# Two-part float16 weights and inputs for the projections, in place of two-part float32r, with the weights scaled by 1024

## The chip, the cores and the metric

The kernel runs on one core of one Trainium2 chip. TensorE (PE in the profile; its weight loads are the row PEld) multiplies, VectorE (DVE) and ScalarE (ACT) work on tiles element by element, GpSimd (POOL) and SyncE (SP) mostly issue transfers (DMA). The metric is the device time of one execution in microseconds (us), the median of several runs.

## The reference, cut to what matters

A sequence of 528 tokens (16 of them meta tokens) with 2048 channels goes through two residual layers. Nearly all of the arithmetic is in four projections, `hn @ w_in` and `... @ w_out` of each layer:

```
for layer in range(DEPTH):                       # DEPTH = 2
    hn = rms_norm(h, norm_gain[layer])
    if layer % 2 == 0:
        y = even_mixer(hn, ...)
    else:
        y = odd_mixer(hn, ...)
    h = h + y
h = rms_norm(h, final_norm_gain)

def even_mixer(hn, w_in, ..., w_out, ...):
    glu_v, glu_g, gate_a, q, c, gate_b, qi, ki, wi = split_last(hn @ w_in, EVEN_SPLITS)
    ...                                          # convolution of width 31; top-k attention of 8 heads
    return jnp.concatenate([a_out, b_out], axis=-1) @ w_out

def odd_mixer(hn, w_in, lb, norm_g, w_out):
    q, fz, i, g = split_last(hn @ w_in, (D_REC, D_REC, D_REC, D_REC))
    ...                                          # gated linear recurrence of 16 heads
    return o @ w_out
```

All inputs and the output are float32.

## The kernel before, in words

**Layout.** Channels lie on the 128 partitions, tokens along the free axis. An input x is 16 tiles of 128 channels by 528 tokens. A weight matrix lies in memory as stripes of 128 output columns; each stripe is two halves of 128 x 1024 float32 (8 blocks of 128 x 128).

**Two parts.** A float32 value is carried as two float32r parts: `hi` is the value as float32r rounds it, `lo` is what is left. For weights `load_half` does it (lines 152 to 161): SP loads a half into `w32` (4 buffers), ACT copies it into `hi` (line 159), DVE subtracts into `lo` (line 160); `wh` and `wl` have 3 buffers each. For inputs `split`, `split2`, `split_tile`, `early_form0`, `gate_form`, `early_form` and `late_form` do the same once per tile. `products` (lines 183 to 191) then multiplies one half: for each of the 8 blocks three products, hi by xh (line 188), hi by xl (line 189) and lo by xh (line 190), all added up in PSUM. A float32r product is one instruction, which loads its own weights; the profile shows the load as a PEld row with the same line.

**Widths.** A stripe over all tokens ("wide") has 2 x 264 columns, one over the 512 tokens without the meta tokens has 512. Three of the projections are done in Strassen's way on blocks of 2 x 2: even output (56 products of one half, 264 columns), and in the odd layer q, part of the gate and the output (147 products of one half, 256 columns). Sums of weight blocks for it are made by adding transfers on POOL's queue (`sum_step`), paced by other work.

**Evacuation.** A wide or narrow stripe leaves PSUM on DVE, multiplied by the row norm (`evac`, line 196). Results of Strassen products are added into their targets on DVE, or copied by ACT (lines 899 to 921, 1034 to 1052, 1395 to 1400 and 1481 to 1512). In the odd layer's Strassen results the norm is multiplied in later (`scaled`, line 991).

**Beside the projections.** While PE multiplies projections, the convolution (line 610, DVE), the choice of the top keys (lines 583 and 584, DVE), attention (lines 675 to 736), and in the odd layer the recurrence of 16 heads (`rec_head`, lines 1148 to 1287) run on the other engines. The recurrence already uses two float16 parts for its small products of 64 columns (lines 1144 to 1146), with weight loads as instructions of their own. Products that are float32 on both sides (transposes, means, attention's values) and the float32r ones of attention's keys (lines 516, 529, 571, 572 and 696) are not part of the projections' path.

**Order.** Each engine works in one fixed order, which a scheduler made from priorities (`band`: weights first, then evacuation, side work, convolution) and its own estimate of times; `issue_after` pins a few places by hand.

**The end.** The last two pairs of output products are followed by the final norm. `final(0)` scales the first 256 tokens group by group (line 1457) into tiles of the pool `r1` (line 1443, 32 of them), which SP sends out, and `final(1)` does the other 256 tokens after the last product.

Of the kernel before, what the change touches and what calls it, by code (L numbers as in the profile page):

```python
# [37 lines left out]
KS, QS = 2.0 ** 14, 1.0  # L38

# [33 lines left out]
def trunk_kernel(ctx: ExitStack, tc: tile.TileContext, x: bass.AP, w: bass.AP, wukv: bass.AP,  # L73
# [78 lines left out]
    def load_half(src, pool=wpool, names=("wh", "wl"), bufs=3, m=128):  # L152
# [6 lines left out]
        halved[:] = [S.activation(uh, used, AF.Copy),  # L159
                     V.tensor_tensor(ul, used, uh.bitcast(F32), op=OP.subtract)]  # L160
# [32 lines left out]
    def evac(dst, parts, rstd):  # L193
        o = T - dst.shape[-1]
        for p, sl in parts:
            V.tensor_tensor(dst[:, sl.start - o:sl.stop - o], p[:dst.shape[0]], rstd[:dst.shape[0], sl],  # L196
                            op=OP.mult)

    def split2(hi, lo, src, scale=1.0):

        if scale == 1.0:
            S.activation(hi, src, AF.Copy)
            V.tensor_tensor(lo, src, hi.bitcast(F32), op=OP.subtract)
        else:
            S.activation(hi, src, AF.Copy, scale=scale)
            V.scalar_tensor_tensor(lo, src, scale, hi.bitcast(F32), op0=OP.mult, op1=OP.subtract)

    def split(pool, src, scale, gname="xh", lname="xl", n=T, bufs=KT):

        xh = pool.tile([128, T], F32R, name=gname, bufs=bufs)  # L210
        xl = pool.tile([128, T], F32R, name=lname, bufs=bufs)
        S.activation(xh[:, T - n:], src, AF.Identity, scale=scale)
        V.scalar_tensor_tensor(xl[:, T - n:], src, scale, xh[:, T - n:].bitcast(F32),
# [134 lines left out]
    def split_tile(k):  # L348
# [3 lines left out]
        xh = r1p.tile([128, T], F32R, name="xh", bufs=KT)  # L352
        xl = r1p.tile([128, T], F32R, name="xl", bufs=KT)
        g = col(V_G0 + k)
        in_turn("a", lambda: S.activation(xh, hin, AF.Identity, scale=g))
        in_turn("v", lambda: V.scalar_tensor_tensor(xl, hin, g, xh.bitcast(F32), op0=OP.mult, op1=OP.subtract))
# [3 lines left out]
    def split_weights(s, half, part=None):  # L360

        m = KWM if s == S_KW else 128
        if part in (None, 0):
            w32 = wpool.tile([128, 1024], F32, name="w32", bufs=4)
            if s == S_KW:
                hi, lo = [et([128, 5, 128], F32, *(("Vt", 3), ("pt", 2))[half]).rearrange("p a b -> p (a b)")
                          .bitcast(F32R) for _ in range(2)]
            else:
                hi, lo = [wpool.tile([128, 1040], F32R, name=n, bufs=3)[:, :1024] for n in ("wh", "wl")]
# [6 lines left out]
        in_turn("a", lambda: S.activation(hi[:, cs], w32[:, cs], AF.Copy))  # L376
        in_turn("v", lambda: V.tensor_tensor(lo[:, cs], w32[:, cs], hi[:, cs].bitcast(F32), op=OP.subtract))
# [71 lines left out]
    with band(SIDE):  # L449
# [4 lines left out]
        V.tensor_scalar(wiT.rearrange("p a b -> p (a b)"), p[:, :NB * NM], 1.0 / 32, None, op0=OP.mult)  # L454
# [30 lines left out]
    with band(SIDE):  # L485
        rc = et([128, T], F32, "acc", 2)
        rstd_from(mean_bcast(ones_d, csq, None), rc, eps_r, et([128, T], F32, "sq", 3), D / 256, eps_c)
        for j in range(2):
            V.scalar_tensor_tensor(cn[j], cn[j], col(V_KV + j), rc, op0=OP.mult, op1=OP.mult)
            CX.append(split(E, cn[j], 1.0, "ch", "cl", bufs=2))  # L490
# [335 lines left out]
    def early_form0(name, src, scale):  # L826
        hi, lo = [xfp.tile([128, HT], F32R, name=n, bufs=24) for n in ("fh", "fl")]
# [8 lines left out]
    with band(SIDE):  # L836
# [6 lines left out]
        for name in ("N2", "N1", "T3", "T4"):  # L843
            for _ in range(4):
                hl = [r1p.tile([128, T], F32R, name=n, bufs=KT) for n in ("xh", "xl")]
# [37 lines left out]
    with band(EVAC):  # L883
# [3 lines left out]
        for n in range(8, KT):  # L887
            residual(n)
    us = [halves_of[p // 2][:, p % 2 * HT:(p % 2 + 1) * HT] for p in range(8)]
    turns = [(p, m) for m in (2, 3, 1, 6, 5, 7, 4) for p in range(8)]  # L890
    for at, (pr, m) in enumerate(turns):
# [5 lines left out]
        with band(EVAC):  # L897
            if m == 2:
                V.tensor_tensor(c0[:, LT], c0[:, LT], o, op=OP.add)
            elif m == 3:  # L900
                V.tensor_tensor(c0[:, RT], c0[:, RT], o, op=OP.add)
            elif m == 1:
                S.activation(u, o, AF.Copy)
                if pr % 3 == 1:
                    paced_steps(lsteps, 1, o, epools["ec"])
                V.tensor_tensor(c0[:, LT], c0[:, LT], o, op=OP.add)
            elif m == 6:
                V.tensor_tensor(u, u, o, op=OP.add)
# [3 lines left out]
            elif m == 5:  # L912
                V.tensor_tensor(c0[:, RT], c0[:, RT], o, op=OP.add)
                V.tensor_tensor(c1[:, RT], c1[:, RT], o, op=OP.subtract)
                finish1(pr)
            elif m == 7:
                V.tensor_tensor(u, u, o, op=OP.add)
                both = c1.rearrange("p (c t) -> p c t", c=2)
                V.tensor_tensor(both, both, u[:, None, :].to_broadcast([128, 2, HT]), op=OP.subtract)
            else:  # L920
                V.tensor_tensor(c1[:, LT], c1[:, LT], o, op=OP.subtract)
# [685 lines left out]
```

## Time and profile before

| what | value |
|---|---|
| median of 3 runs | 1862.81 us (1862.80 to 1863.81) |
| profiled execution | span 1859.9 us from its first to its last instruction; the page gives no other time of it, so the 2.9 us up to the median are taken as what lies around the span |
| mean granted TensorE clock | 0.998 |
| busy share of DVE, ACT, POOL | 81%, 51%, 14% |
| float32r projection products of 128 x 1024 halves, three lines | 12,552 of the lines 188 to 190, and 192 of the lines 412 to 414 |
| weight halves split on ACT and DVE (lines 159 and 160) | 376 |
| bytes moved by DMA | 379.64 MB, 204 GB/s over the span |

How to read it: PE's records overlap, since a product's record lasts some 280 ns while the next starts after some 120 ns. So what a product costs is the distance from one start to the next in a stream without gaps, and not the length of its record; the timeline gives these starts. On DVE and ACT a record's length is close to the cost (neighbouring records overlap a little). The chain that ended last tells which engine's work fills the span.

### The profile page before, as it was taken

The page shows a single profiled execution, that of the slowest core. Times are in us where ns is not written, and L with a number is a line of the kernel's source. Part 1 is how long each engine was busy: PE and PEld are TensorE (multiplying, and loading weights), DVE is VectorE, ACT ScalarE, POOL GpSimd, SP SyncE. Part 2 cuts the span into 40 slices and gives each one's busy share as a digit, 9 for nine tenths or more (in the row PEclk, how much of TensorE's full clock was granted, in tenths as well). Part 3 has the DMA queues.
Part 4 walks back from the last instruction along what each step waited for, and adds up shares of the span by engine and source line. Part 5 has one row for each costly group of instructions (what it writes and reads, how often), then busy time and mean ns, then how long its engine had stood idle before and what let it go on. Part 6 is the DMA issues. An engine that isn't in the chain of part 4 may idle for free.

```text
span 1859.9 us, 39100 instructions
## 1 busy us (share of the span) xinstructions
PE 1847.7 (99%) x15739; PEld 1804.7 (97%) x15739; DVE 1498.6 (81%) x2898; ACT 945.1 (51%) x1719; POOL 264.9 (14%) x469
## 2 busy tenths in 40 slices
PE   9999999999999999999999999999999999999997
PEld 9998899999999999999999999999999999989997
DVE  7699799998658579588876667999899888869777
ACT  6333532234443655456644455766556656546653
POOL 1120132123331212010000001011101110000000
PEclk9999999999999999999999999999999999999999
DMA  7478777988996867786889886655555455325665
GB/s 283 145 245 257 194 230 191 246 219 204 235 262 207 205 196 251 219 264 235 242 253 288 270 252 207 183 155 159 148 152 167 123 159 141 111 94 161 218 223 170
DMA packets 106020, 379.64 MB, mean 204 GB/s; under 512 B 15472, under 2 KB 23320, under 8 KB 103984
## 3 DMA queue, kind: packets, MB, share of 16 engines
q1 hardware_dynamic: 71872, 232.68, 36.4%
q0 software_dynamic: 33680, 144.28, 32.6%
q8 instruction: 123, 2.02, 0.4%
q14 instruction: 57, 0.47, 0.1%
q10 hardware_dynamic: 288, 0.19, 0.0%
HBM read 354.26 MB, written 136.53 MB: 264 GB/s over the span
## 4 chain that ended last, share of the span: by engine, by line
PE 98%; DVE 1%; ACT 0%; DMA 0%; issue 0%; SPq 0%; DVEq 0%
PE mps L188 22%; PE mps L189 22%; PE mps L190 22%; PE s L189 3%; PE s L188 3%; PE s L190 3%; PE sv L189 2%; PE sv L190 2%; PE sv L188 2%; PE st L189 1%; PE st L188 1%; PE st L190 1%; PE po L724 1%; PE s L1144 1%; PE po L1267 1%; PE s L1146 1%
## 5 line engine op out<-in xcount | busy, mean ns | idle before, releaser
L188 PE MATMUL mps<-xh,wh 128*128 128x264 f32 (+2 forms) x2840 | 837.1, 295 | 0.0
L189 PE MATMUL mps<-xl,wh 128*128 128x264 f32 (+2 forms) x2840 | 835.8, 294 | 0.0
L190 PE MATMUL mps<-xh,wl 128*128 128x264 f32 (+2 forms) x2840 | 835.7, 294 | 0.0
L159 ACT ACTIVATE wh<-w 128x1024 fp32r<-128x1024 f32 x376 | 398.5, 1060 | 535.9 <-PE mps L189 351.0
L160 DVE TENSOR_TENSOR wl<-w,wh 128x1024 fp32r<-128x1024 f32 x376 | 459.7, 1223 | 159.9 <-ACT wh L159 155.3
L189 PEld LDWEIGHTS mps<-xl,wh 128*128 128x128 f32 x2840 | 535.0, 188 | 9.2
L188 PEld LDWEIGHTS mps<-xh,wh 128*128 128x128 f32 x2840 | 534.7, 188 | 9.3
L190 PEld LDWEIGHTS mps<-xh,wl 128*128 128x128 f32 x2840 | 534.6, 188 | 9.2
L610 DVE SCALAR_TENSOR_TENSOR z<-u,vec,z 128x528 f32<-128x528 f32 x240 | 180.9, 763 | 2.4
L260 POOL DMA_DIRECT2D ws<-in_w_dram x116 | 104.6, 1108 | 119.4 <-DMA ws<-ws 69.7
L189 PE MATMUL s<-xl,wh 128*128 128x256 f32 (+1 forms) x288 | 81.4, 283 | 0.0
L188 PE MATMUL s<-xh,wh 128*128 128x256 f32 (+1 forms) x288 | 81.4, 282 | 0.0
L190 PE MATMUL s<-xh,wl 128*128 128x256 f32 (+1 forms) x288 | 80.9, 281 | 0.0
L1227 DVE COPY_PREDICATED A<-msk,s 128x256 f32<-128x256 uint8 x96 | 47.0, 489 | 10.2 <-PE s L1146 9.7
L189 PEld LDWEIGHTS s<-xl,wh 128*128 128x128 f32 x288 | 54.2, 188 | 0.7 <-issue 0.6
L190 PEld LDWEIGHTS s<-xh,wl 128*128 128x128 f32 x288 | 54.3, 189 | 0.0
L188 PEld LDWEIGHTS s<-xh,wh 128*128 128x128 f32 x288 | 54.3, 188 | 0.0
L673 POOL DMA_DIRECT2D L<-mask x32 | 31.8, 993 | 148.6 <-DMA L<-bdram 75.6
L1140 ACT ACTIVATE qhm<-q 128x256 f16<-128x256 f32 x96 | 38.4, 416 | 26.2 <-DVE q L1242 16.1
L1140 ACT ACTIVATE kt0h<-k 128x512 f16<-128x512 f32 (+1 forms) x64 | 33.1, 517 | 32.7 <-DVE k L1233 27.0
L196 DVE TENSOR_TENSOR gt<-mps,rstd 128x264 f32<-128x264 f32 (+1 forms) x70 | 31.4, 450 | 21.3 <-PE mps L190 21.0
L302 POOL MEMSET pace<- 128x1 f32 x36 | 3.9, 108 | 298.2 <-ACT pace L301 298.2
(764 smaller groups left out, 4060.1 us busy)
## 6 DMA issues: line engine op xcount, KB each, us to landing
w<-in_w_dram SPq DMA_DIRECT2D x262, 512.0 KB, 4.4
ws<-in_w_dram POOLq DMA_DIRECT2D x158, 512.0 KB, 7.8
w<-ws SPq DMA_DIRECT2D x116, 512.0 KB, 4.3
ws<-ws POOLq DMA_DIRECT2D x58, 512.0 KB, 5.5
ws<-in_w_dram SPq DMA_DIRECT2D x16, 512.0 KB, 7.1
on<-h1d SPq DMA_DIRECT2D x30, 256.0 KB, 4.1
sq<-mbd POOLq DMA_DIRECT2D x16, 264.0 KB, 3.2
qd<-on SPq DMA_DIRECT2D x12, 256.0 KB, 5.4
```

The costliest lines, as they stand in the source:

```text
L159: halved[:] = [S.activation(uh, used, AF.Copy), V.tensor_tensor(ul, used, uh.bitcast(F32), op=OP.subtract)]
L160: V.tensor_tensor(ul, used, uh.bitcast(F32), op=OP.subtract)]
L188: P.matmul(o, hi[:, ws], xh, start=start and k == 0, stop=False)
L189: P.matmul(o, hi[:, ws], xl, start=False, stop=False)
L190: issued.append(P.matmul(o, lo[:, ws], xh, start=False, stop=stop and k == len(X) - 1))
L196: V.tensor_tensor(dst[:, sl.start - o:sl.stop - o], p[:dst.shape[0]], rstd[:dst.shape[0], sl], op=OP.mult)
L260: return G.dma_start(wsum[pair, m], src, accum_op=OP.add, max_dma_last_dim=4096)
L610: V.scalar_tensor_tensor(z, u[:, j:j + T], col(V_CW + i * CW + j), z, op0=OP.mult, op1=OP.add)
L673: return G.dma_start(biased[h, t][:, :wk(t)], M[t], accum_op=OP.add)
L724: P.matmul(o[:, 128 * t:128 * (t + 1)], Vt[:, j, :], pt[:, j, :], start=j == 0, stop=j == t + 1)
L1140: S.activation(hi, src, AF.Copy, scale=scale)
L1227: V.copy_predicated(A.rearrange("p b (n a m) -> p b n a m", a=2, m=mm)[:, :, :, 1, :], msk[:, li - 1 + i:li + i, :].rearrange("p b (n m) - ...
```

## The change

Both parts of the projections' weights and inputs become float16. Weights are multiplied by 1024 as they are split (`WS`, in ACT's copy and in DVE's subtraction, which becomes SCALAR_TENSOR_TENSOR), and each place that reads a projection's result out of PSUM multiplies by 1/1024 (`IW`). Inputs of the projections are split into float16 without a further scale. The keys and values of attention (`CX`, `kih`, `qa`) stay float32r.

```
+WS = 2.0 ** 10
+IW = 1.0 / WS
...
-        hi = pool.tile([128, wide], F32R, name=names[0], bufs=bufs)[:, :1024]
-        lo = pool.tile([128, wide], F32R, name=names[1], bufs=bufs)[:, :1024]
+        hi = pool.tile([128, wide], F16, name=names[0], bufs=bufs)[:, :1024]
+        lo = pool.tile([128, wide], F16, name=names[1], bufs=bufs)[:, :1024]
...
-        halved[:] = [S.activation(uh, used, AF.Copy),
-                     V.tensor_tensor(ul, used, uh.bitcast(F32), op=OP.subtract)]
+        halved[:] = [S.activation(uh, used, AF.Copy, scale=WS),
+                     V.scalar_tensor_tensor(ul, used, WS, uh, op0=OP.mult, op1=OP.subtract)]
...
     def evac(dst, parts, rstd):
...
-            V.tensor_tensor(dst[:, sl.start - o:sl.stop - o], p[:dst.shape[0]], rstd[:dst.shape[0], sl],
-                            op=OP.mult)
+            V.scalar_tensor_tensor(dst[:, sl.start - o:sl.stop - o], p[:dst.shape[0]], IW,
+                                   rstd[:dst.shape[0], sl], op0=OP.mult, op1=OP.mult)
...
+    def gain(to, ps, by=IW):
+        return V.scalar_tensor_tensor(to, ps, by, to, op0=OP.mult, op1=OP.add)
...
-                V.tensor_tensor(c0[:, LT], c0[:, LT], o, op=OP.add)
+                gain(c0[:, LT], o)
...
-                o = r1p.tile([128, T], F32R, name=("xh", "xl")[g % 2], bufs=KT).bitcast(F32)
+                o = fp.tile([128, 2 * HS], F32, name="oc", bufs=4)
```

The other splits (`split`, `split2`, `split_tile`, `split_weights`, `early_form0`, `gate_form`, `early_form`, `late_form`) change their tiles from F32R to F16 in the same way, and the other additions of results become `gain`. Lines shift: 160 of before is 162 now, 188 to 190 are 190 to 192, 196 is 198, 583 and 584 are 589 and 590, 610 is 616, and 1144 to 1146 are 1153 to 1155.

**On PE**, a float16 product does not load its own weights: a LDWEIGHTS instruction stands ahead of each. Here is a place in the recurrence before, where PE comes back from a short float16 pair of a head (`kt0h` holds that head's keys, `s_14878` is its PSUM tile) to the projections:

```order
L1144 LDWEIGHTS kt0h
L1144 MATMUL s_14878<-qlm,kt0h 128x64
L1145 LDWEIGHTS kt0h
L1145 MATMUL s_14878<-qhm,kt0h 128x64
L189 MATMUL mps<-xl,wh 128x264
L190 MATMUL mps<-xh,wl 128x264
L188 MATMUL mps<-xh,wh 128x264
L189 MATMUL mps<-xl,wh 128x264
```

The same return in another head, of the changed kernel:

```order
L1153 LDWEIGHTS kt0h
L1153 MATMUL s_14399<-qlm,kt0h 128x64
L1154 LDWEIGHTS kt0h
L1154 MATMUL s_14399<-qhm,kt0h 128x64
L190 LDWEIGHTS wh
L190 MATMUL mps<-xh,wh 128x264
L191 LDWEIGHTS wh
L191 MATMUL mps<-xl,wh 128x264
L192 LDWEIGHTS wl
L192 MATMUL mps<-xh,wl 128x264
```

The projections now have the same form as the short products beside them, and 12,744 LDWEIGHTS are added (14,280 in all, 1,536 before); the number of products stays at 15,392. There are 58 such returns in the order before and 59 now. The side work stands at nearly the same place among the projections: from the top-k scores to the end of attention at the very same product, elsewhere within some 60 products.

**On DVE**, the order stays as it was through nearly all of the even layer's attention and convolution. Here is a piece of before from the stretch where convolution (`z`), choice of the top keys (`mask`), weight splits (`wl`) and evacuation (`gt`) share the engine:

```order
L160 TENSOR_TENSOR wl<-w_3757,wh 128x1024
L610 SCALAR_TENSOR_TENSOR z<-u,vec,z 128x528
L584 MATCH_REPLACE mask_703<-m_2970,mask_703 128x272
L610 SCALAR_TENSOR_TENSOR z<-u,vec,z 128x528
L196 TENSOR_TENSOR gt<-mps,rstd 128x264
L583 MAX m_2973<-mask_703 128x8
```

The same place in the changed kernel:

```order
L162 SCALAR_TENSOR_TENSOR wl<-w_3757,wh 128x1024
L616 SCALAR_TENSOR_TENSOR z<-u,vec,z 128x528
L590 MATCH_REPLACE mask_703<-m_2970,mask_703 128x272
L616 SCALAR_TENSOR_TENSOR z<-u,vec,z 128x528
L198 SCALAR_TENSOR_TENSOR gt<-mps,rstd 128x264
L589 MAX m_2973<-mask_703 128x8
```

Only the operation of the split and of the evacuation has changed. Over the program 701 TENSOR_TENSOR of DVE become SCALAR_TENSOR_TENSOR. ACT has the same instructions and two more loads of an activation table (11 for 9), because some small operations of the odd layer's set-up (lines 1103 to 1124 of before) now stand earlier, among the even layer's output products.

More of the change, by code (lines that the diff above doesn't have):

```diff
@@ L202, in split2, with split @@
             S.activation(hi, src, AF.Copy)
[L203 removed]
+            V.tensor_tensor(lo, src, plain(hi), op=OP.subtract)
         else:
             S.activation(hi, src, AF.Copy, scale=scale)
[L206 to L211, printed above, removed]
+            V.scalar_tensor_tensor(lo, src, scale, plain(hi), op0=OP.mult, op1=OP.subtract)
+    def split(pool, src, scale, gname="xh", lname="xl", n=T, bufs=KT, dt=F16):
+        xh = pool.tile([128, T], dt, name=gname, bufs=bufs)
+        xl = pool.tile([128, T], dt, name=lname, bufs=bufs)
         S.activation(xh[:, T - n:], src, AF.Identity, scale=scale)
[L213 removed]
+        V.scalar_tensor_tensor(xl[:, T - n:], src, scale, plain(xh[:, T - n:]),
                                op0=OP.mult, op1=OP.subtract)
@@ L366, in split_weights @@
                 hi, lo = [et([128, 5, 128], F32, *(("Vt", 3), ("pt", 2))[half]).rearrange("p a b -> p (a b)")
-                          .bitcast(F32R) for _ in range(2)]
+                          .bitcast(F16)[:, :640] for _ in range(2)]
             else:
-                hi, lo = [wpool.tile([128, 1040], F32R, name=n, bufs=3)[:, :1024] for n in ("wh", "wl")]
+                hi, lo = [wpool.tile([128, 1040], F16, name=n, bufs=3)[:, :1024] for n in ("wh", "wl")]
             first[s, half] = hi, lo
@@ L826, in early_form0 @@
     def early_form0(name, src, scale):
-        hi, lo = [xfp.tile([128, HT], F32R, name=n, bufs=24) for n in ("fh", "fl")]
+        hi, lo = [xfp.tile([128, HT], F16, name=n, bufs=24) for n in ("fh", "fl")]
         split2(hi, lo, src, scale)
@@ L844, in trunk_kernel @@
             for _ in range(4):
-                hl = [r1p.tile([128, T], F32R, name=n, bufs=KT) for n in ("xh", "xl")]
+                hl = [r1p.tile([128, T], F16, name=n, bufs=KT) for n in ("xh", "xl")]
                 forms0[name] += [[t[:, c] for t in hl] for c in (LT, RT)]
@@ L1317, in early_form @@
     def early_form(name, i, src):
-        both = fp.tile([128, 2 * HS], F32R, name=f"{name}{i}", bufs=1)
+        both = fp.tile([128, 2 * HS], F16, name=f"{name}{i}", bufs=1)
         hi, lo = both[:, :HS], both[:, HS:]
@@ L1325, in late_form @@
         if i % 2 == 0:
-            late[name] = [r1p.tile([128, T], F32R, name=n, bufs=KT) for n in ("xh", "xl")]
+            late[name] = [r1p.tile([128, T], F16, name=n, bufs=KT) for n in ("xh", "xl")]
         sl = slice(i % 2 * HS, (i % 2 + 1) * HS)
```

57 lines of the change are left out of this document (30 added, 27 removed).

## The prediction, made before the changed kernel had run

> **What bounds the kernel now.** I read the page's head first, then the chain that ended last, then what PE waited for.
>
> ```profile
> span 1859.9 us, 39100 instructions
> PE 1847.7 (99%) x15739; PEld 1804.7 (97%) x15739; DVE 1498.6 (81%) x2898; ACT 945.1 (51%) x1719; POOL 264.9 (14%) x469
> ...
> PEclk9999999999999999999999999999999999999999
> ...
> PE 98%; DVE 1%; ACT 0%; DMA 0%; issue 0%; SPq 0%; DVEq 0%
> ```
>
> PE fills 98% of the chain at a clock that is never throttled. The list of PE's waits has three entries in all:
>
> ```profile
> PE mps L139 <- DVE ones_d L124: 1.1, 1, 1.1
> PE po L1433 <- DVE rstd L1415: 0.5, 1, 0.5
> PE mps L413 <- DVE xl L356: 0.4, 1, 0.4
> ```
>
> 2 us of waits in 1860: PE is the bound from the first 30 us to the last 12. A busy PE is no proof of that, since its records overlap; that it never waits is. So the distance from one product's start to the next sets the time. Two windows of 100 us hold nothing but projections, the first of 264 columns, the second of 256 (columns: PE, PEld, DVE, ACT, POOL busy with instructions, clock, DMA share, GB/s):
>
> ```profile
> 700.00:800.00 100.00, 100.00 (x826) 100.00 (x825) 75.92 (x133) 49.22 (x82) 14.23 (x28) 1.00 0.78 240
> 1000.00:1100.00 100.00, 100.00 (x853) 100.00 (x853) 59.57 (x75) 44.30 (x68) 9.06 (x24) 1.00 0.87 268
> ```
>
> 100/826 is 0.121 us for 264 columns, 100/853 is 0.117 us for 256. For 512 columns the timeline has 28 products in a row, 27 distances in 6.27 us, 0.232 us each:
>
> ```profile
> 1665.65 0.40 PE L189 MATMUL mps<-xl,wh 128*128 128x512 f32 x1
> ...
> 1671.92 0.40 PE L189 MATMUL mps<-xl,wh 128*128 128x512 f32 x1
> ```
>
> **The products.** How many of each there are follows from the code: 73 wide stripes of 96, 56 Strassen products of 24, and 192 at the start (96 of them with 80 weight columns) make 8,544 of 264 columns; 147 Strassen products of 24 make 3,528 of 256; 14 stripes of 48 make 672 of 512. What will a float16 product of these widths cost? The trace has float16 pairs, load and product, of 64 columns, here between projections:
>
> ```profile
> 1172.84 0.28 PE L190 MATMUL mps<-xh,wl 128*128 128x264 f32 x1
> ...
> 1173.56 0.28 PE L190 MATMUL mps<-xh,wl 128*128 128x264 f32 x1
> ...
> 1173.73 0.19 PE L1144 MATMUL s<-qlm,kt0h 128*128 128x64 f16 x1
> ...
> 1174.31 0.19 PE L1146 MATMUL s<-qhm,kt0l 128*128 128x64 f16 x1
> 1174.34 0.37 PE L188 MATMUL mps<-xh,wh 128*128 128x264 f32 x1
> 1174.55 0.28 PE L189 MATMUL mps<-xl,wh 128*128 128x264 f32 x1
> ```
>
> From 1173.73 to 1174.31 lie 20 distances, 0.029 us each, with a weight load in every one. That is at most 0.455 ns a column if nothing of it is fixed: the upper bounds are 0.1196 us for 264 columns, 0.116 for 256, 0.232 for 512. For the lower bound I take the plain float32 products:
>
> ```profile
> 590.74 0.45 PE sv L224 x2
> 591.19 0.45 PE s L224 x2
> ...
> 468.24 0.44 PE st L717 x4
> 468.67 0.11 PE s L721
> ```
>
> The rows of L224 have 264 columns and take 0.225 us each; L717 has 128 and takes (468.67-468.24)/4 = 0.1075. Both are 0.84 to 0.85 ns a column, twice what the float16 rows allow, so I read them as columns that pass the array twice, at 0.42 ns (an inference from the ratio). One pass of 264 columns is then 0.111 to 0.1125 us, 256 are 0.1075, 512 are 0.215. A float32r product of 256 columns at 0.117 is slower than two passes of 128 at 0.1075, so something in float32r costs about a tenth beyond the columns. I take values at the lower bounds, being nearest in the number of columns that pass: **0.112, 0.109 and 0.217 us**. The saving is 8,544 x 0.009 = 77 us, 3,528 x 0.008 = 28 us, 672 x 0.015 = 10 us, together **115 us**. By the upper bounds it is 8,544 x 0.0014 + 3,528 x 0.001 = 15 us, by the lower ones 8,544 x 0.010 + 3,528 x 0.0097 + 672 x 0.017 = 131 us.
>
> [...]
>
> **The weight loads.** 12,744 loads become instructions of their own.
>
> ```profile
> L188 PEld LDWEIGHTS mps<-xh,wh 128*128 128x128 f32 x2840 | 534.7, 188 | 9.3
> L1145 PEld LDWEIGHTS <-kt0h 128*128 128x128 f16 x256 | 23.3, 99 | 0.4 <-issue 0.2
> ```
>
> A float16 load's record is 99 ns against 188, and in the pairs above it hides behind a product of only 64 columns; behind 256 it has more room. I cost it at nothing; the cover is the product ahead. Where float32r follows a short float16 product the load isn't covered: 1174.34 to 1174.55 is 0.21 us, 0.09 over the stream. The order has 58 such returns; with float16 weights that excess should go: 58 x 0.09 = **5 us**.
>
> **DVE and ACT.** The split changes from TENSOR_TENSOR to SCALAR_TENSOR_TENSOR with float16 on one input and the output, and evacuations get an immediate factor. The trace has both forms at equal sizes, from SBUF (512 columns) and from PSUM (256), and for ACT the copy into float16 and into float32r:
>
> ```profile
> L160 DVE TENSOR_TENSOR wl<-w,wh 128x1024 fp32r<-128x1024 f32 x376 | 459.7, 1223 | 159.9 <-ACT wh L159 155.3 <-PE mps L190 0.6
> L1141 DVE SCALAR_TENSOR_TENSOR kt0l<-k,kt0h 128x512 f16<-128x512 f32 x32 | 22.0, 686 | 2.2 <-ACT kt0h L1140 2.2
> L1275 DVE TENSOR_TENSOR sl<-so,sh 128x512 fp32r<-128x512 f32 x16 | 11.0, 689 | 0.0
> L1052 DVE SCALAR_TENSOR_TENSOR on<-on,s 128x256 f32<-128x256 f32 x9 | 3.8, 418 | 1.1 <-PE s L190 0.9
> L1040 DVE TENSOR_TENSOR on<-on,s 128x256 f32<-128x256 f32 x7 | 2.9, 420 | 1.7 <-PE s L190 1.5
> L1140 ACT ACTIVATE kt0h<-k 128x512 f16<-128x512 f32 x32 | 20.0, 624 | 15.5 <-DVE k L1233 13.4 <-PE s L1146 1.8
> L1273 ACT ACTIVATE sh<-so 128x512 fp32r<-128x512 f32 x16 | 10.0, 626 | 0.2
> ```
>
> 686 against 689, 418 against 420, 624 against 626 ns: no difference, 0 us. Then the same DVE work stands in a shorter time. ACT's two more table loads fall where ACT is half idle (700:800 above): nothing, with the three buffers of weights as cover.
>
> **Where DVE becomes late.** L160's row says that DVE's idle time is mostly waiting for `wh`, which waits for PE to free a buffer: slack that PE's pace makes. It is not spread evenly.
>
> ```profile
> 100.00:200.00 100.00, 100.00 (x595) 89.17 (x594) 93.60 (x143) 34.72 (x63) 15.03 (x26) 1.00 0.80 233
> 240.00:340.00 100.00, 100.00 (x826) 99.86 (x825) 94.54 (x231) 29.28 (x56) 24.04 (x38) 1.00 0.81 215
> 340.00:440.00 100.00, 100.00 (x830) 99.86 (x830) 93.22 (x169) 36.56 (x74) 26.69 (x40) 1.00 0.87 223
> 1200.00:1300.00 100.00, 100.00 (x1086) 98.58 (x1083) 95.18 (x235) 64.22 (x127) 12.46 (x22) 1.00 0.52 146
> 1300.00:1400.00 100.00, 100.00 (x1067) 98.61 (x1066) 91.23 (x224) 57.14 (x110) 11.77 (x21) 1.00 0.53 149
> ```
>
> DVE is idle for 6.4, 5.5, 6.8, 4.8 and 8.8 us of 100. PE wants to save 0.009/0.121 = 7.4% of its projection time, 6 to 7 us of 100 there (some PE time is other work). If 2.5 us of idle in 100 can't be used (waits in DVE's own chains), PE falls short by some 3, 3.5, 2.5, 4.5 and 0.5 us, 14 in all. A lead of two weight halves (2 x 48 x 0.121 = 12 us) absorbs a part. I take **10 us** of new waits, and as bounds 0 and 42 (no saving at all in these five windows and the next one, 6 x 7). DMA's share, up to 0.87 here, rises by a fifteenth; no PE wait before came from it, and the four `w32` buffers hold 23 us of lead. I cost it at nothing.
>
> **The end.** Tiles for the first half's output come from 4 buffers, not 32: the fifth group waits until the first is sent. Its bound is one transfer, 2 us; I take 0, as the groups come in two bursts, around the last products.
>
> **Sum.** 115 + 5 - 10 = 110 us less. Of the profiled execution that leaves 1859.9 - 110 = 1749.9 us; the median is 2.9 us above that span, so **1752.8 us**.
>
> **Rivals.** (1) DVE takes the bound in the dense stretches and all its idle time there is needed: the six windows keep their length, 42 us of the saving go, and with 115 + 5 - 42 = 78 us less it is **1785**. For it: 95% busy. Against it: much of the idle time waits on PE. (2) The columns cost 0.455 ns in float16 too, so that the change hardly does what its shorter operands suggest: 15 us less, **1848**. The plain float32 rows speak against it. (3) The rate is a property of these shapes and not of the type: no change, **1863**. The 0.029 us row speaks against that only for short products. (4) The slower one: loads are covered while products alternate in a small tile, but not in long streams, so each of the 12,744 products pays for its load. From 115/12,744 = 9 ns a load it is slower than before. The rows' largest price is the whole float16 pair, 29 ns: 12,744 x (29 - 9) = 255 us more, **2118**. Against it: the load's time is inside the 29 ns.
>
> [...]
>
> **How the numbers follow.** Forecast 0.80, rival 1 0.10, rival 2 0.04, rival 3 0.03, rival 4 0.03. The forecast's own range goes from 1733 (lower bounds of the product, 131 + 5 - 6 us) to 1775 (the waits tripled); with rival 1 it reaches **1733 to 1790**, which leaves out rivals 2 to 4 and some of the forecast's edges. A measurement of this kernel tells 0.2% (4 us) from no change. Faster by more: 0.94; within: 0.03; slower: 0.03.
>
> **What would show it.** Right: windows of nothing but projections with 890 products in 100 us (264 columns) and 915 (256); 0.12 us after a float16 pair and not 0.21; L162 still at 1.22 us; DVE above 85% busy; a few PE waits on `wl` or on PSUM in the five windows. Wrong: 835 products in 100 us (rival 2), PE waits of over 30 us on DVE (rival 1), records of loads that begin only when the product ahead has ended (rival 4).

## The result

| | before | after |
|---|---|---|
| median | 1862.91 us (1862.80 to 1863.81, 4 runs) | 1763.63 us (1762.75 to 1763.84, 4 runs) |
| ratio | | 0.9463, 95% interval 0.9449 to 0.9476 |
| profiled execution, span | 1859.9 us | 1760.6 us |

The time fell by 99.3 us, in the medians as in the two profiled spans; 110 were forecast. The page of the changed kernel begins so (span, busy time of each engine, the clock granted to PE in 40 slices, the chain that ended last):

```profile
span 1760.6 us, 39044 instructions
...
PE 1731.9 (98%) x15739; PEld 1466.3 (83%) x15739; DVE 1481.5 (84%) x2898; ACT 944.4 (54%) x1721; POOL 264.8 (15%) x469
...
PEclk9999999999999999999999999999999999999998
...
PE 78%; DVE 11%; DMA 4%; issue 4%; ACT 1%; POOL 0%; SPq 0%; DVEq 0%; POOLq 0%; ACTq 0%
```

PE is still the bound, but its share of the chain went from 98% to 78%: DVE and DMA now end waits of PE. Windows of 100 us (busy time and instructions of PE, PEld, DVE, ACT, POOL, then clock, DMA share and GB/s) show what it gained and where it stands still:

```profile
700.00:800.00 100.00, 98.52 (x872) 84.75 (x870) 80.04 (x129) 56.90 (x83) 13.64 (x24) 1.00 0.83 253
900.00:1000.00 100.00, 99.25 (x910) 88.72 (x909) 69.64 (x95) 43.52 (x64) 10.01 (x26) 1.00 0.90 284
...
340.00:440.00 100.00, 99.95 (x879) 88.49 (x878) 99.13 (x182) 40.24 (x89) 26.17 (x39) 1.00 0.87 241
1100.00:1200.00 100.00, 100.00 (x1129) 89.18 (x1128) 98.33 (x239) 72.62 (x139) 12.15 (x20) 1.00 0.62 173
1200.00:1300.00 100.00, 100.00 (x1141) 89.49 (x1141) 98.65 (x247) 64.00 (x125) 13.78 (x24) 1.00 0.61 169
```

872 products of 264 columns in 98.52 us are 0.113 us each, 910 of 256 in 99.25 are 0.109. In the last three windows DVE is busy for 98 to 99 us of 100, and PE waits there for 0.05 us of 300. The group of DVE's weight splits (count, busy us, mean ns, idle time before them and what ended it):

```profile
L162 DVE SCALAR_TENSOR_TENSOR wl<-w,wh 128x1024 f16<-128x1024 f32 x376 | 458.4, 1220 | 130.2 <-ACT wh L161 127.9
```

The split takes 1220 ns where it took 1223. The timeline at a return from a short float16 pair in the recurrence:

```profile
1111.60 0.19 PE L1153 MATMUL s<-qlm,kt0h 128*128 128x64 f16 x1
1111.63 0.19 PE L1154 MATMUL s<-qhm,kt0h 128*128 128x64 f16 x1
1111.66 0.28 PE L190 MATMUL mps<-xh,wh 128*128 128x264 f16 x1
1111.78 0.28 PE L191 MATMUL mps<-xl,wh 128*128 128x264 f16 x1
```

The first projection product behind the pair takes 0.12 us, not 0.21. And here are the longer entries of PE's list of waits, which had three entries in all before the change (total, times, longest, in us), then the largest entry of the weight loads' list:

```profile
PE mps L190 <- DVE gt L198: 3.0, 1, 3.0
PE s L192 <- DVE wl L162: 2.4, 3, 1.2
PE st L522 <- DVE st L707: 1.8, 1, 1.8
PE mps L192 <- DVE wl L162: 1.7, 2, 1.1
PE sv L192 <- DVE wl L162: 1.6, 2, 1.1
```
```profile
PEld L192 <- DVE wl L162: 10.4, 14, 1.5
```

To put numbers on places, I took each distance between the starts of neighbouring PE products, and against it the usual distance of the first one's form (0.121 us for 264 columns in float32r, 0.1125 in float16, and so on). The usual distances add up to 1829.9 us before and 1715.3 after, **114.6 us less**. What lies above them, in us, for both kernels and for two versions that come up below (each in its own time, stages put side by side):

| stage (us, after) | before | after | gate forms held | and evictions first |
|---|---|---|---|---|
| start, to 50 | 4.7 | 5.8 | 5.6 | 5.4 |
| 50 to 450 | 1.5 | 3.4 | 3.1 | 3.1 |
| 450 to 500 | 0.3 | 3.9 | 2.1 | 2.0 |
| 500 to 750 | 1.3 | 1.7 | 1.7 | 1.5 |
| 750 to 900 | 0.4 | 6.6 | 0.0 | 0.0 |
| 900 to 1100 | -0.7 | 1.8 | -0.1 | -0.1 |
| recurrence, 1100 to 1600 | 11.0 | 8.9 | 10.8 | 5.9 |
| the rest | 0.4 | 2.1 | 2.1 | 2.5 |
| sum | 18.9 | 34.0 | 25.4 | 20.3 |

114.6 less and 15.1 more are 99.5, the 99.3 us of the spans within what such a tally can hold (another choice of the usual distances moves the sums by about 1 us). In the recurrence 11.0 fell to 5.9 once a wait of 3 us at its end is taken away (last column), so the returns brought 5.1. The returns themselves, taken alone, agree: behind a short float16 pair, the distances after the first projection product lie 4.9 us above the usual in all before (58 returns) and less than 0.1 us after (59). The new waits are then 15.1 + 5.1 = **20 us**, and the places of the larger ones are at 465, 776 to 848, 998, 1015 and 1565 us.

### The profile page after: what moved, and what is told of

Its sections match the earlier page's. It is cut to its first block, busy times and chain, and to the rows that moved or that the text cites. A ratio compares the mean times of both kernels' runs of the same rounds, so it can differ in the third digit from the quotient of the medians.

```text
span 1760.6 us, 39044 instructions
## 1 busy us (share of the span) xinstructions
PE 1731.9 (98%) x15739; PEld 1466.3 (83%) x15739; DVE 1481.5 (84%) x2898; ACT 944.4 (54%) x1721; POOL 264.8 (15%) x469
## 4 chain that ended last, share of the span: by engine, by line
PE 78%; DVE 11%; DMA 4%; issue 4%; ACT 1%; POOL 0%; SPq 0%; DVEq 0%; POOLq 0%; ACTq 0%
PE mps L190 17%; PE mps L192 17%; PE mps L191 17%; DVE wl L162 3%; PE s L192 2%; PE s L191 2%; PE s L190 2%; DVE z L616 1%; DVE mask L590 1%; DMA L<-mask 1%; PE sv L192 1%; PE sv L190 1%; PE sv L191 1%; DVE m L589 1%; DMA w<-in_w_dram 1%
## 5 line engine op out<-in xcount | busy, mean ns | idle before, releaser
L190 PE MATMUL mps<-xh,wh 128*128 128x264 f16 (+2 forms) x2840 | 806.8, 284 | 3.1 <-DVE gt L198 3.0
L192 PE MATMUL mps<-xh,wl 128*128 128x264 f16 (+2 forms) x2840 | 806.8, 284 | 1.7 <-DVE wl L162 1.7
L191 PE MATMUL mps<-xl,wh 128*128 128x264 f16 (+2 forms) x2840 | 806.9, 284 | 0.0
L161 ACT ACTIVATE wh<-w 128x1024 f16<-128x1024 f32 x376 | 396.1, 1054 | 422.7 <-PE mps L191 266.2
L162 DVE SCALAR_TENSOR_TENSOR wl<-w,wh 128x1024 f16<-128x1024 f32 x376 | 458.4, 1220 | 130.2 <-ACT wh L161 127.9
L192 PEld LDWEIGHTS <-wl 128*128 128x128 f16 x4184 | 409.6, 98 | 90.8 <-DVE wl L162 10.4
L191 PEld LDWEIGHTS <-wh 128*128 128x128 f16 x4184 | 409.7, 98 | 82.8 <-issue 5.0
L190 PEld LDWEIGHTS <-wh 128*128 128x128 f16 x4184 | 409.6, 98 | 81.2 <-issue 2.7
L192 PE MATMUL s<-xh,wl 128*128 128x256 f16 (+1 forms) x288 | 78.9, 274 | 1.6 <-DVE wl L162 1.6
L191 PE MATMUL s<-xl,wh 128*128 128x256 f16 (+1 forms) x288 | 78.8, 274 | 0.0
L190 PE MATMUL s<-xh,wh 128*128 128x256 f16 (+1 forms) x288 | 78.8, 274 | 0.0
L198 DVE SCALAR_TENSOR_TENSOR gt<-mps,rstd 128x264 f32<-128x264 f32 (+1 forms) x70 | 31.2, 448 | 14.5 <-PE mps L192 14.4
```

What stands on the lines that cost most here:

```text
L161: halved[:] = [S.activation(uh, used, AF.Copy, scale=WS), V.scalar_tensor_tensor(ul, used, WS, uh, op0=OP.mult, op1=OP.subtract)]
L162: V.scalar_tensor_tensor(ul, used, WS, uh, op0=OP.mult, op1=OP.subtract)]
L190: P.matmul(o, hi[:, ws], xh, start=start and k == 0, stop=False)
L191: P.matmul(o, hi[:, ws], xl, start=False, stop=False)
L192: issued.append(P.matmul(o, lo[:, ws], xh, start=False, stop=stop and k == len(X) - 1))
```

## The experiments

Two things had to be told apart: is the gain PE's pace alone, and what are the 20 us? The first theory was that DVE's order and its three buffers of weights are behind them; the rival that DVE is simply too slow for the new pace.

### The arithmetic without the type

```
-        hi = pool.tile([128, wide], F16, name=names[0], bufs=bufs)[:, :1024]
+        hi = pool.tile([128, wide], F32R, name=names[0], bufs=bufs)[:, :1024]
...
-                     V.scalar_tensor_tensor(ul, used, WS, uh, op0=OP.mult, op1=OP.subtract)]
+                     V.scalar_tensor_tensor(ul, used, WS, uh.bitcast(F32), op0=OP.mult, op1=OP.subtract)]
```

> The arithmetic of the change without its type: weights scaled by 2^10, the three-operand forms at every split and eviction, but all tiles of the projections float32r again. Theory (the whole gain is the 0.0326 ns that a column of a product streams faster, the new forms cost and bring nothing): 1863 us within 4, the 264-column product at 0.121 again, DVE's weight split at 1.22 us. Rival (part of the gain comes from the new forms or from the scaling): 5 us or more below 1863. Rival (the new forms cost DVE something that the change hides): 5 us or more above.

1862.89 us, ratio 0.9996 (0.9987 to 1.0006). A window of it, and DVE's split:

```profile
700.00:800.00 100.00, 100.00 (x826) 100.00 (x825) 76.09 (x133) 48.88 (x82) 14.23 (x28) 1.00 0.75 240
```
```profile
L162 DVE SCALAR_TENSOR_TENSOR wl<-w,wh 128x1024 fp32r<-128x1024 f32 x376 | 459.4, 1222 | 160.1 <-ACT wh L161 155.5 <-PE mps L192 0.6
```

826 products again, as before the change. Scale, three-operand forms and evictions bring nothing and cost nothing; the whole gain comes with the type.

### Another type of two bytes

The same kernel with `BF = mybir.dt.bfloat16` in place of `F16` in the projections' tiles.

> The changed kernel with bfloat16 in place of float16 for both parts (fewer bits are kept; nothing is left out). Theory (the pace follows the width of two bytes, not the format): 264 columns at 0.1125 us, 256 at 0.109, and 1763 us within 4. Rival (float16 has a pace of its own): another distance, and 15 us or more away.

1759.42 us, ratio 0.9443 (0.9426 to 0.9460), and in a window of 256 columns:

```profile
900.00:1000.00 100.00, 100.00 (x918) 89.63 (x916) 71.78 (x97) 44.22 (x63) 10.09 (x26) 1.00 0.94 292
```

100/918 is 0.109 us: the same pace. The 4 us below the changed kernel are just at the edge of what was expected. They aren't the products: PE's wait at 465 us was 1.0 us here instead of 2.0, and from 900 to 1100 us it has no wait (916 to 918 products in 100 us, 908 to 910 in the changed kernel). So where waits fall was worth 4 us between two builds with the same pace, and differences of that size below are not leaned on without the trace.

### Every weight loaded twice

```
+            P.ldweights(hi[:, ws])
             P.matmul(o, hi[:, ws], xh, start=start and k == 0, stop=False)
+            P.ldweights(hi[:, ws])
             P.matmul(o, hi[:, ws], xl, start=False, stop=False)
+            P.ldweights(lo[:, ws])
```

> The changed kernel with one more weight load (the same columns) issued ahead of nearly every product of the projections, some 12,500 loads in all, none of which changes a result. Theory (a load runs beside the product before it and costs nothing while it is shorter than the product, 98 ns in its record against 112 us per thousand products): within 10 us of 1763. [...] Middle (two loads of 98 ns don't fit beside one product of 112 ns, so that a product's distance becomes 196 ns): about 2700 us.

1785.26 us, ratio 0.9584 (0.9565 to 0.9603): 21.6 us more, outside the 10 that the theory gave, and far from the 2700 us of two loads that don't fit beside one product. A window:

```profile
900.00:1000.00 100.00, 99.50 (x913) 99.30 (x1822) 69.41 (x93) 45.02 (x66) 9.35 (x26) 1.00 0.90 293
```

913 products stand beside 1,822 loads, where 910 stood beside 909: in a long stream a second load costs nothing either, though two records of 98 ns don't fit one after the other beside 0.109 us (the records overlap: the timeline has them start 0.04 to 0.07 us apart). The 21.6 us lie in places. The largest is a wait for the attention's mask at 459 us:

```profile
PEld st L525 <- DVE st L710: 8.3, 1, 8.3
```

That is 6.8 us more between 450 and 500 us than in the changed kernel, by the tally above. Some 5 us lie between 1630 and 1660, in pauses of half a us; the rest is spread. Why PE pauses there was not settled.

### DVE without the weights' second part

```
-        halved[:] = [S.activation(uh, used, AF.Copy, scale=WS),
-                     V.scalar_tensor_tensor(ul, used, WS, uh, op0=OP.mult, op1=OP.subtract)]
-        return hi, lo
+        halved[:] = [S.activation(uh, used, AF.Copy, scale=WS)] * 2
+        return hi, hi
```

> The changed kernel without DVE's split of the streamed weights: the first part is loaded in the second's place, so that the weights' second part is left out and DVE has some 370 instructions of 1.22 us, 450 us, less to do; PE's products are the same in number and shape. Theory (PE is the bound and what DVE costs now is the waits that are new, some 20 us of which DVE ends 15): 1743 to 1752 us. Rival (DVE bounds whole stretches of the changed kernel): below 1735. Rival (the waits are not DVE's): 1758 or more.

1759.89 us, ratio 0.9444 (0.9430 to 0.9458): 3.7 us less than the changed kernel, with 27% of DVE's work gone. By the number this is the second rival, but its waits are of another kind. PE's list, then DVE's:

```profile
PE st L700 <- DVE st L705: 10.3, 1, 10.3
PE s L721 <- ACT L L712: 2.1, 1, 2.1
```
```profile
DVE L L705 <- DMA L<-mask: 20.5, 4, 10.0
```

No wait on a split is left, nor the one at 1565 us; in their place PE waits once for 10.3 us at 309 us, since DVE's softmax there waits for the mask that an accumulating transfer adds to the bias (`L<-mask`). So DVE doesn't bound whole stretches, and there is a second suspect, DMA. The tally gives the price of both: the stretch with the mask, 50 to 450 us, lies 16 us higher than in the changed kernel (waits of 10.3 and 2.3 us, and a granted clock of 0.89 on average from 300 to 360 us), all others together 19 us lower. So without DVE's splits the waits fell by about what the theory said, and a new one took most of that back.

### The gate forms back in their place

DVE's waits bunch between 760 and 860 us. There the two kernels differ in the order of DVE. The odd layer's `gate_forms` (lines 954 to 975 of before) make forms of `h1d`, read back from DRAM. Before, the first of them ran on DVE right behind the last `finish1` (876.2 us, behind 875.6). With the change it runs at 772.1 us, 105 of DVE's instructions ahead of the last `finish1` (842.6 us), and 20 more of the forms' instructions run ahead of that too. What DVE then did (start, duration, and in brackets the idle time ahead and what ended it):

```profile
814.89 0.42 DVE L896 SCALAR_TENSOR_TENSOR z<-mps,z 128x264 f32<-128x264 f32 x1
819.18 0.48 DVE L975 SCALAR_TENSOR_TENSOR on<-on,vec,on 128x256 f32<-128x256 f32 x1 [3.88 <-DMA on<-h1d]
819.59 1.22 DVE L162 SCALAR_TENSOR_TENSOR wl<-w,wh 128x1024 f16<-128x1024 f32 x1
```

A form that nobody needs for another 60 us waits 3.88 us for its transfer, and the split that PE needs next stands behind it. The experiment holds the forms behind the last `finish1`:

```
...
-    with band(SIDE):
+    with band(SIDE), tc.issue_after(last.ins), tc.issue_after(summed[0].ins):
         for i in range(8):
             gate_forms(i)
```

Here `last` is ACT's last instruction of `finish1` and `summed[0]` DVE's.

> The changed kernel, with the odd layer's gate forms held, on ACT and DVE, behind the last finish1 of the early half, as they stood in the kernel before. Theory (some 6.5 us of the new waits, between 750 and 850 us, come from these forms having moved ahead on DVE, where a form of h1d waits 3.9 us for its transfer and the weight splits queue behind it): 1757 us, and no wait of PE on a weight split between 760 and 860 beyond 1 us. Rival (DVE is just too slow for PE's new pace there, whatever the order): 1763 us, the same waits at other instructions. Rival (the forms come late for the gates then): above 1765.

1753.57 us (1751.89 to 1758.03), ratio 0.9413 (0.9396 to 0.9430), below the changed kernel's interval. The window from 760 to 860 us, of the changed kernel and then with the forms held:

```profile
760.00:860.00 100.00, 95.06 (x831) 80.57 (x829) 91.78 (x159) 65.69 (x101) 8.72 (x16) 1.00 0.77 251
```
```profile
760.00:860.00 100.00, 100.00 (x892) 87.27 (x890) 95.38 (x162) 69.32 (x108) 9.80 (x19) 1.00 0.78 264
```

Three more instructions on DVE, 95% busy, and PE no longer waits at all. The 10 us are more than the 6.5 expected: of the 8.6 us by the tally 6.6 went here, 1.9 between 900 and 1100 and 1.8 at 465, while 2.0 came at the recurrence's end, where the clock was 0.89 on average from 1550 to 1565 us, against 1.00 from 1560 to 1575 in the changed kernel (below). Only the 6.6 us are the order's for certain. Of those at 465 the wait itself has only 0.2 (1.6 us, 1.8 in the changed kernel); the rest lies behind it, where the products came every 0.11 us with the forms held and every 0.22 us, at a clock of 0.50, in the changed kernel. Those between 900 and 1100 are missing also from bfloat16 and from the next run, in both of which the forms run as early as in the changed kernel.

### Why they had moved: memory

```
-        hi, lo = [gpp.tile([128, HS], F16, name=n, bufs=32) for n in ("gh", "gl")]
+        hi, lo = [gpp.tile([128, 2 * HS], F16, name=n, bufs=32)[:, :HS] for n in ("gh", "gl")]
```

> The changed kernel with the gate forms' tiles (gh, gl) allocated at twice their width, so that they take the bytes that float32r took, and only the first half of each used; no order is prescribed. Theory (the forms moved ahead on DVE since the smaller tiles leave their space free earlier): they begin after the last finish1 again, near 830 us in the new time, the waits on the weight split between 760 and 860 us go, and the time is that of the kernel with the forms held, 1752 to 1758 us. Rival (the scheduler moved them for another reason, as the pace of PE): they still begin near 772 us, 1763.

The theory's order did not come about: by the view of the tile `gl`, its first form still ran at 773.1 us.

```profile
L960 DVE SCALAR_TENSOR_TENSOR gl<-n,vec,gh x8: 477/490/502, 773.1 to 862.5; 128x256 f16<-128x256 f32 x8
```

The time, 1756.80 us (0.9435, 0.9420 to 0.9451), came out in the theory's range all the same, but not by the theory: waits of 1.2 us are left at 786 and 820 us, and the tally still has some 5 us between 750 and 900, 1.5 less than the changed kernel. The rest of the 6.8 us lies elsewhere: 1.8 between 900 and 1100, 1.6 at 465 and 1.0 in the recurrence. What brought these was not shown, and the early order keeps its price. The next run gave the same room to all tiles of the inputs and forms, `xh` and `xl` first of all, below which the gate forms' pool lies:

```
-        xh = r1p.tile([128, T], F16, name="xh", bufs=KT)
-        xl = r1p.tile([128, T], F16, name="xl", bufs=KT)
+        xh = r1p.tile([128, 2 * T], F16, name="xh", bufs=KT)[:, :T]
+        xl = r1p.tile([128, 2 * T], F16, name="xl", bufs=KT)[:, :T]
...
-        hi, lo = [gpp.tile([128, HS], F16, name=n, bufs=32) for n in ("gh", "gl")]
+        hi, lo = [gpp.tile([128, 2 * HS], F16, name=n, bufs=32)[:, :HS] for n in ("gh", "gl")]
```

> The changed kernel with every float16 tile of the inputs and forms (xh, xl, fh, fl, gh, gl) allocated at twice its width, half of it used, so that memory is laid out as with float32r; no order is prescribed. The run with gh and gl alone at twice their width still had the forms early (770 us). Theory (it is the sum of the smaller tiles, those of the inputs below and of the gate forms themselves, that leaves the forms' space free while the early half still runs): the forms begin after the last finish1, near 828 us, the waits on the weight split between 760 and 860 us fall below 1 us, and the time is that of the kernel with the forms held, 1752 to 1757 us. Rival (the order alone doesn't decide, what ran early costs little; the runs with forms held were faster by chance of the clock): 1758 to 1764 us.

1753.48 us (0.9408, 0.9394 to 0.9422). The same view, then the window:

```profile
L959 DVE SCALAR_TENSOR_TENSOR gl<-n,vec,gh x8: 476/479/483, 832.9 to 867.4; 128x256 f16<-128x256 f32 x8
```
```profile
760.00:860.00 100.00, 100.00 (x890) 87.20 (x889) 94.82 (x161) 68.58 (x106) 9.70 (x18) 1.00 0.80 261
```

No order was prescribed, and the forms went back behind `finish1`. So the smaller tiles themselves undid a wait that had kept the order good. I read it so that with float32r the forms' memory was taken until the early half was done; which tile held it was not traced.

### Six buffers of weights

```
-    def load_half(src, pool=wpool, names=("wh", "wl"), bufs=3, m=128):
+    def load_half(src, pool=wpool, names=("wh", "wl"), bufs=6, m=128):
```

The two other places that make `wh` and `wl` change alike.

> The changed kernel with six buffers instead of three for the weights' two parts (wh, wl), which float16 leaves room for. Theory (DVE can be late for a few us at a time since only three halves are split ahead; it isn't the bound over a whole stretch): the 12 us of PE's waits on DVE's weight split fall below 3, 1754 us. Rival (the splits are late because their data or DVE's order are, not for want of a buffer): 1761 to 1764, the waits stay. The load of w32 has four buffers as before, so a wait on the transfer may come in their place.

1756.20 us (1750.34 to 1760.78), ratio 0.9421 (0.9398 to 0.9444). Every wait on `wl` is gone from PE's list, as the theory has it, and others stand there (the profiled execution is the slowest of the four, 1760.78 us):

```profile
PE st L522 <- DVE st L707: 3.2, 1, 3.2
PE mps L190 <- DVE gt L198: 3.0, 1, 3.0
PE sv L723 <- ACT L L714: 2.7, 1, 2.7
```

The second stood there before. The first and the third are the attention's softmax, at 467 and 299 us. With both edits:

> The gate forms held and six buffers for wh and wl together. Theory (the two take away different waits: DVE's order near 800 us, and splits that are a few us late at 299, 687 and 998 us): 1749 to 1752 us. Rival (the deeper buffers let the weights' transfers run ahead and make the mask late, as the run with six buffers alone showed at 299 and 467 us with 2.9 and 3.4 us): 1753 to 1758 us, PE's waits at these two places longer than with the forms held alone, and runs that differ by some us.

1755.26 us (0.9421, 0.9407 to 0.9435), no better than the forms held alone. By the number that is the rival, but not by its mechanism: PE's waits at 299 and 465 us were 1.0 and 1.8 us, about as long as with the forms held alone (0.9 and 1.8). Once the order is right, deeper buffers bring nothing that the time shows.

### The mask that lands late

What is left before 500 us hangs on `L<-mask`. The softmax's instruction on DVE ahead of PE's wait at 465 us, in the changed kernel:

```profile
465.52 0.43 DVE L707 CUSTOM_DVE_ANT_0 L<-s,L 128x264 f32<-128x264 f32 x1 [3.97 <-DMA L<-mask]
```

The view of transfers between 440 and 470 us of the changed kernel (queue, count, size, median us from issue to landing):

```profile
ws<-in_w_dram POOLq DMA_DIRECT2D x7, 512.0 KB, 12.1
...
L<-mask POOLq DMA_DIRECT2D x1, 264.0 KB, 14.9
```

The mask's transfer, 6.2 us in its median, takes 14.9 among seven transfers for sums of weights (`ws`) on the same queue. Two runs, both with the forms held. In the first, the mask is issued ahead of the sums:

```
                 if t:
-                    mask = mask_ahead(h + 1, t - 1)
-                    behind = behind if h else mask
+                    behind = mask_ahead(h + 1, t - 1)
+                if t == NB - 1:
+                    behind = mask_ahead(h + 1, t)
                 some_steps(steps, (2, 2, 2, 3)[t] if h == 0 else (2, 2, 1, 2)[t] if h < 6 else 1, behind)
-                if t == NB - 1:
-                    mask_ahead(h + 1, t)
```

> The kernel with the gate forms held, and the attention's mask (264 KB, L<-mask) issued on POOL's queue ahead of the weight sums (ws, 512 KB each) that stand before it now. Theory (the waits of PE at 299 and 465 us come from the mask's landing behind these transfers, 15.8 us after its issue where its median is 6; the faster PE reaches that point before it lands): PE's wait for st at 465 falls from 1.6 us below 0.5, no half-speed stretch of PE's clock behind it, 1749 to 1752 us. Rival (the transfers are late whatever their order, since the 16 DMA engines are busy over 90% there): 1753 to 1755, the wait moves to another transfer.

1776.28 us (0.9531, 0.9514 to 0.9547), 23 us slower than with the forms held; neither theory had that. POOL's and DVE's waits:

```profile
POOL L L679 <- DMA L<-bdram: 132.9, 22, 16.2
```
```profile
DVE L L707 <- DMA L<-mask: 41.6, 11, 8.2
```

POOL now stands still until the bias has landed, 133 us in all where it was 79 with the forms held, and what stands behind in its order starts later; DVE's waits for the mask go from 10.4 to 41.6 us. The edit mended one transfer (10.1 us instead of 15.8) and made eleven waits where there were three. In the second run the sums' accumulating transfers are left out:

```
-        return G.dma_start(wsum[pair, m], src, accum_op=OP.add, max_dma_last_dim=4096)
+        return dst_of[0]
```

> The kernel with the gate forms held, without the accumulating transfers of the weight sums (the second addend of each sum of weights, L265, is left out, so that these weights are those of one matrix alone), which takes over a hundred transfers of 512 KB off POOL's queue; every product, split and eviction stays. Theory (what is left of PE's new waits before 500 us, at 299 and 465 us, is the attention's mask landing late among these transfers): both gone, DVE's wait for L<-mask below 3 us in all where the kernel with the forms held has 10.4, 1748 to 1751 us. Rival (the chain from bias over mask to softmax is too long by itself for the faster PE): the waits stay, 1752 to 1756 us.

1752.48 us (0.9401, 0.9385 to 0.9417), outside the theory's range and within the rival's. The transfers between 440 and 470 us:

```profile
L<-mask POOLq DMA_DIRECT2D x1, 264.0 KB, 3.8
```

The mask lands after 3.8 us, DVE no longer waits for it, the wait at 465 is gone (0.2 us between 450 and 500 in the tally, from 2.1), that at 299 is down to 0.4 from 0.9. So these transfers make the mask late, as the theory has it; whether by their place in the queue or by the load on the DMA engines, the run can't tell, since it takes away both. The price isn't the theory's, since 2.3 us of waits on `wl` came up between 677 and 684 us (0.8 before); what makes these splits late was not traced. In the time the two versions can't be told apart.

### The wait at 1565 us

The largest single wait is one for an eviction. DVE, with the forms held, where this stage is 10 us earlier:

```profile
1551.30 0.69 DVE L1285 TENSOR_TENSOR sl<-so,sh 128x512 fp32r<-128x512 f32 x1
1555.78 1.23 DVE L162 SCALAR_TENSOR_TENSOR wl<-w,wh 128x1024 f16<-128x1024 f32 x1 [3.79 <-ACT wh L161]
1557.02 0.69 DVE L1296 TENSOR_TENSOR on<-po,rs 128x512 f32<-128x512 f32 x1
1557.63 1.28 DVE L198 SCALAR_TENSOR_TENSOR gt<-mps,rstd 128x512 f32<-128x512 f32 x2
```

It is a ring. DVE's two evictions (L198) free the tiles that PE needs (it waits for them for 3.0 us); they stand behind a split (L162), which waits for ACT's `wh`, which waits until PE is done with an older one. The run puts the last head's multiplication (L1296) behind these evictions, and the order follows:

```
...
+        if h == 11:
+            with band(SIDE), tc.issue_after(evacuated.ins):
+                V.tensor_tensor(ON[15], summed[1], ON[15], op=OP.mult)
```

> The kernel with the gate forms held, and at the recurrence's end the last head's multiplication by rs put behind the first two evictions of the gates, whose results PE needs freed: on DVE's row these two evictions (L198) now stand ahead of a weight split (L162), which waits 3.8 us for ACT, and ahead of that multiplication, which waits for ACT's rs. Theory (PE's wait of 3.2 us near 1555 us and the half-speed stretch of 2 to 3 us behind it are only this order): both gone, 1748 to 1751 us. Rival (PE then waits for something else there, as wh, wl or the square root's chain): 1752 to 1754 us.

1749.56 us (1747.92 to 1753.57, 5 runs), ratio 0.9397 (0.9384 to 0.9410). DVE there:

```profile
1551.34 1.28 DVE L198 SCALAR_TENSOR_TENSOR gt<-mps,rstd 128x512 f32<-128x512 f32 x2
1552.54 1.09 DVE L1392 TENSOR_TENSOR t<-on 128x256 f32<-128x256 f32 x3
1555.21 1.23 DVE L162 SCALAR_TENSOR_TENSOR wl<-w,wh 128x1024 f16<-128x1024 f32 x1 [1.58 <-ACT wh L161]
```

The evictions run at 1551 instead of 1558, PE's wait is gone, and with it the clock's loss (1.00 from 1550 to 1565 us, 0.89 with the forms held): 4.9 us less in the recurrence by the tally. In the times alone this version and that with the forms held can't be told apart, since their intervals overlap; the trace decides. This version is 14 us below the changed kernel and 114 below the one before.

## Why the prediction was right, and where it was not

**The products.** 115 us were predicted, 114.6 came. The distances are those chosen, 0.112 and 0.109 us (872 and 910 products in their windows), so the float32 rows, halved, gave the right size; that float32 passes the array twice is not shown by it. The run with the type put back shows that nothing else took part, and bfloat16 that it is not float16's own pace. For 256 and 512 columns the prediction took 0.109 and 0.217, a little above the 0.1075 and 0.215 that it had from the float32 rows, and no run before the change shows them; the changed kernel's streams gave 0.109 and 0.216.

**The weight loads.** Nothing, as predicted: 909 loads beside 910 products. Twice the loads, 1,822 beside 913 products, left the stream as it was.

**The returns.** 5 us predicted; 5.1 by the tally, 4.9 counted at the returns alone, 0.12 us behind a short pair in the timeline.

**DVE's and ACT's new forms.** Nothing predicted; 1220 against 1223 ns, and 1862.89 us with these forms alone.

**The new waits** are the step that was off: 10 us predicted, 20 came, and most of them not where the prediction put them. It took DVE's idle time as too little in five dense windows, with 2.5 us of idle in 100 that can't be used. There PE lost almost nothing: from 1100 to 1300 us it has no wait with DVE idle for 1.4 to 1.7 us of 100, and in the two windows from 240 to 440 the tally has some 2 us. A busy share of 98% did no harm, since the work came in an order that suited PE. What cost time was order: forms moved ahead (6 to 7 us between 750 and 900), a ring around an eviction (3 us at 1565), and the mask among other transfers (2 us of wait at 465, and some 1.7 more, an estimate, by 3.41 us at a clock of 0.50 behind it). Two single waits of 0.9 us at 998 and 1015 have no shown cause, and some 5 us lie spread over the other stages. The prediction compared PE's order closely and DVE's not at that place, though the move could be seen in the order of DVE's instructions before any run. That the time came out in the range all the same is owed to the range, which left room for three times the waits, and not to where it put them.

**DMA** was costed at nothing, since no wait of PE had come from it. DVE's had: the softmax waited 6.9 us for the mask before the change, 2.6 us at the longest, out of PE's sight. After it the sum is 6.3 us, but one wait is 4.0, and PE stands behind it.

**The rivals.** DVE as the bound would have cost 42 us and given 1785. Leaving its largest work out gave 1759.89, and without the new wait for the mask some 19 us less than the changed kernel (an estimate from the tally), so it was not near. The rivals with less or no gain fell with the products, that of the uncovered loads with the doubled ones.

**The sum.** 115 + 5 - 10 = 110 against 114.6 + 5.1 - 20 = 99.7: the 10 us by which the time was missed are the waits, nothing else. With the two orders mended the time is 1749.56 us, 3 below the forecast. The end, taken as nothing, cost nothing: 10.3 us from the last product's start to the end of the span before, 10.4 after. One sign failed narrowly: DVE is busy for 84%, not above 85%. Two figures of the working are off without touching the forecast: 0.029 / 64 is 0.453 ns a column, not 0.455, and the waits tripled give 1773, not 1775. And of its two float32 rows that of L717 is a transpose.

## What to carry over

A change of an operand's type changes the size of its tiles, and a scheduler that waited for memory may then start work earlier than is good: compare the order of every engine, not only of the one that gains. An engine at 98% need not cost anything beside the bound (DVE from 1100 to 1300 us, where PE waited for nothing), while one instruction that waits for a transfer, ahead of what the bound needs next, can cost its whole wait (3.88 us on DVE at 815 us; PE lost 4.1 between 812 and 835). When the bound gets faster, look for waits of the other engines that were hidden until then.

## What was not expected of the hardware

**PE's clock was halved behind a wait of 2 us, and not behind one of 3 us.** In the changed kernel PE stood still for 2 us at 465 us:

```profile
464.97 0.28 PE L191 MATMUL mps<-xl,wh 128*128 128x264 f16 x1
467.03 0.39 PE L522 MATMUL st<-ch,uh 128*128 128x264 f32 x1 [1.78 <-DVE st L707]
...
468.46 0.43 PE L191 MATMUL mps<-xl,wh 128*128 128x264 f16 x1
468.68 0.43 PE L192 MATMUL mps<-xh,wl 128*128 128x264 f16 x1
```

Then, 1.4 us after it went on, its products took 0.22 us each instead of 0.1125. The window view gives the granted clock: for the stretch with this wait and the one behind it, and for the two stretches on which the wait of 3.0 us at 1565 us falls:

```profile
465.00:468.42 3.42, 1.64 (x14) 1.28 (x12) 1.96 (x7) 1.41 (x3) 0.29 (x1) 1.00 1.04 283
468.42:471.83 3.41, 3.41 (x18) 2.77 (x17) 1.22 (x1) 1.33 (x4) 2.03 (x3) 0.50 1.09 222
1564.10:1567.51 3.41, 1.67 (x8) 0.83 (x7) 1.28 (x2) 2.36 (x4) 0.00 (x0) 1.00 0.10 40
1567.51:1570.93 3.42, 2.14 (x10) 0.97 (x10) 3.42 (x9) 3.40 (x11) 0.00 (x0) 1.00 0.66 236
```

The clock was 1.00 through the wait at 465 us and 0.50 for the 3.41 us behind it. That cost some 1.7 us (an estimate: 3.41 us at half pace), so this wait of 2 us cost nearly twice its length. The longer wait was followed by no loss: the clock is 1.00 in both of its stretches and up to the last products. PE is idle for 1.74 and 1.28 us in these two stretches and for 1.78 us in the one at 465. With the forms held it was the other way round. Behind its wait of 1.6 us at 465 the products came every 0.11 us, but behind that of 3.0 us at 1555 products of 512 columns came every 0.43 us from 1558.6 to 1561.6, where they had come every 0.216, and the clock from 1550 to 1565 us was 0.89 on average. What decides whether a loss of clock follows was not shown. Versions with much the same waits can so differ by some 1.7 us at one place (the estimate above).

**float32r streamed a fifteenth slower than float16**, in proportion to the columns: 0.121 against 0.1125 us for 264, 0.117 against 0.109 for 256 and 0.232 against 0.216 for 512. bfloat16 had 0.109 for 256 too. So it is not a fixed price for each load; what in float32r costs it was not tried.
